# One 512-column product in place of two of 256 columns in the last feed-forward

## The chip, the cores and the metric

The kernel runs on one core of a Trainium2 chip. The metric is the device time of one execution in microseconds (us). A program of this kind repeats within about 0.1%: the three runs of the kernel before lie between 2305.07 and 2306.84 us. A nanosecond (ns) is a thousandth of a microsecond; durations of single instructions are given in ns.

The engines are named as the profile names them: PE is TensorE's matrix product and PEld its weight load, DVE is VectorE, ACT is ScalarE, POOL is GpSimd, SP is SyncE, whose queue here issues the DMAs.

## The reference

A two-layer trunk works on two groups of 128 tokens of width 2048, a context pass and a denoising step, with the same weights. Each layer is a mixer (attention) followed by a gated feed-forward with a width-3 convolution over the tokens. The change is in the feed-forward of the second, last layer:

```
def conv_ffn(h, w_up, w_conv, b_conv, w_down):
    u = h @ w_up                                   # 2048 -> 2 * 5632
    up = jnp.pad(u, ((0, 0), (1, 1), (0, 0)))
    u = up[:, :-2] * w_conv[0] + up[:, 1:-1] * w_conv[1] + up[:, 2:] * w_conv[2] + b_conv
    gate, val = u[..., :D_FF], u[..., D_FF:]
    return (jax.nn.silu(gate) * val) @ w_down      # 5632 -> 2048
...
x = x + gt2 * conv_ffn(h, ...)
```

All of it is float32.

## The kernel before

The two groups lie side by side: every product has 2 x 128 = 256 token columns (`NT`), and features stand on the 128 partitions. A weight matrix is cut into blocks of 128 x 128. One output chunk of 128 features is the sum over all blocks of its row of weights: 16 blocks for the up-projection (2048 inputs), 22 for one half of the down-projection (the 5632 inputs are done in two halves, `NQ = 2`).

A product in full float32 is made of three products in a faster format, `fp32r`. Each weight is split into a high part `wh` (ACT casts it, L248) and the rest `wl` (DVE subtracts, L249), and so is each operand: its high half lies in columns 0 to 255 of a 512-column row, its low half in columns 256 to 511. `gemm` then adds three products of 256 columns for each block into one PSUM tile `acc` of 128 x 512, of which it uses the first half: `wh` times the high half, `wh` times the low half, `wl` times the high half. Every product loads its weights anew. `acc` has three buffers, `raw` (the weights as they come from memory, 1 MB) three, `wh` and `wl` four each, every one with 8 blocks.

`ffn` runs, for each half `q` of the 5632 features, `up(q)` and then `down(gs, q)`. `up` takes 22 pairs of chunks (gate and value). `conv` asks `product()` for a chunk and makes the convolution of it: ACT scales and shifts it out of PSUM into `cv` (L1531), and DVE adds the two neighbours with two operations that read PSUM (L1534, L1537). Then ACT takes the SiLU of the gate, DVE multiplies (L1554), and the result is split into the high and low half of `g`. `down` makes 16 chunks of 22 blocks each, and `residual` (L843) or, for the very last chunk, `last_residual` (L827) adds them to `x` with DVE, straight from PSUM.

In the last feed-forward the first four chunks of `up` are ready before: they were made from the raw operand while the norm's factor was still being computed, three products of 258 columns to a block ("raw chunks"). `product()` hands them out first. Then come some chunks in an order written out by hand (`in_order`, with `keep_order`), and then five chunks whose first product is widened by 32, 16, 8, 4 and 2 columns (`WIDER`), the extra columns being thrown away. All the others use plain `gemm`.

Beside the products of `up(0)` DVE also works through rows of `w_ada` for the modulation vectors: long reductions at L473, which `pump` hands out at a rate (`FRATE`). The order of instructions on each engine is otherwise set by a scheduler with its own timing model, from the order of the code.

At the end, after the last chunk of `down(1)`, the last squares, the norm's factor and the scaling of `x` follow, one after the other, and the output goes out.

Of the kernel before, what the change touches and what calls it, by code (L numbers as in the profile page):

```python
# [14 lines left out]
ALU = mybir.AluOpType  # L15
# [3 lines left out]
P = 128  # L19
# [3 lines left out]
NT = 2 * T  # L23
ROW = 2 * NT
SHIFT = 320
NL = 2
# [68 lines left out]
def step_kernel(ctx: ExitStack, tc: tile.TileContext, A: dict):  # L95
    nc = tc.nc
    dve, act, pool, sp = nc.vector, nc.scalar, nc.gpsimd, nc.sync
    kept = []

    def keep_order(i):  # L100
        if not any(i is j for j in kept):
            kept[:] = [i]
            tc.keep_in_program_order(i)
# [16 lines left out]
    pe = TensorE()  # L120
# [5 lines left out]
    pacc = ctx.enter_context(tc.tile_pool(name="pacc", bufs=3, space=PSUM))  # L126
# [5 lines left out]
    def banks(name):  # L132
        return tc.tile_pool(name=name, bufs=1, space=PSUM)
# [3 lines left out]
    def nm(s):  # L137
        uid[0] += 1
        return f"{s}_{uid[0]}"

    def T_(pl, shape, tag, dt=F32, bufs=None):
        kw = {} if bufs is None else {"bufs": bufs}
        return pl.tile(shape, dt, tag=tag, name=nm(tag), **kw)
# [103 lines left out]
    def split(out_hi, out_lo, src, pin=lambda i: i):  # L247
        pin(act.copy(out_hi, src))  # L248
        pin(dve.tensor_tensor(out=out_lo, in0=src, in1=out_hi.bitcast(F32), op=ALU.subtract))  # L249
# [102 lines left out]
        return [p[:, :NT] for p in ps]  # L352

    push = []

    def gemm(blocks, xh, xl, n=NT, first=0, between=None, more=None, wider=None):

        fixed = lambda i: keep_order(i) if between is not None else i  # L360
        ps = T_(pacc, [P, 512], "acc")
        last = len(blocks) - 1
        for i in range(last + 1):
            k = (i + first) % (last + 1)
            wh, wl = blocks[k]
            x0 = more(k) if more and i == 0 else wider(k, 0, n + push.pop(0)) if push else xh(k)
            fixed(pe.matmul(ps[:, :x0.shape[-1]], wh, x0, start=(i == 0), stop=False,
                            skip_group_check=i > 0 and x0.shape[-1] > n))
            if callable(between):
                if i == (last + 1) // 2:  # L370
                    between()
            elif between and i in between:
                between[i]()
            x1 = wider(k, NT, n + push.pop(0)) if push else xl(k)
            fixed(pe.matmul(ps[:, :x1.shape[-1]], wh, x1, start=False, stop=False, skip_group_check=x1.shape[-1] > n))
            fixed(pe.matmul(ps[:, :n], wl, xh(k), start=False, stop=(i == last)))
        return ps[:, :n]
# [81 lines left out]
    def load_row():  # L459
        feat["row"] = T_(feat["home"], [P, 2, D], "condb")  # L460
        sp.dma_start(out=feat["row"], in_=A["condb"])
        for r in range(2):
            keep_order(act.activation(feat["row"][:, r], feat["row"][:, r], AF.Silu))
# [30 lines left out]
    class Deep:  # L494
# [44 lines left out]
        def pump(self):  # L539
            self.due += self.rate  # L540
            while self.due >= 1.0:
                self.due -= 1.0
                if self.steps:
                    self.step()
# [82 lines left out]
    def ensure(l, j, qs=range(4)):  # L627
        for u in [(l, j, q) for q in qs]:
            while u in ROWS and u not in done and ada["i"] <= ROWS.index(u):
                row_step()  # L630
            while u in FEATS and u not in done:
                feature_step()
            while u in DEEP[l] and u not in done:
                deep.step()
            while u not in done:
                later.pop(0)()
# [95 lines left out]
    def raw_tile(pl, tag):  # L732
        return home(pl, tag)[:, :KD * 2 * UW].rearrange("p (k n) -> p k n", k=KD)
# [766 lines left out]

    def ffn(hx, W, ready, turn, l, st):
        xh, xl = (lambda k: hx[:, k, :NT]), (lambda k: hx[:, k, NT:2 * NT])
        wider = list(WIDER)
        long = len(ready) > 3

        def product():
            if ready:
                return ready.pop(0)
            if in_order:
                return gemm(W.chunk(), xh, xl, between=in_order.pop(0))  # L1510
            if wider:
                n = NT + wider.pop(0)
                return gemm(W.chunk(), xh, xl, more=lambda k: hx[:, k, :n])
            return gemm(W.chunk(), xh, xl)

        WD = Weights(A["w_down"][l], KQ, TB)
        cw = ada["cw"]
        with tc.tile_pool(name=f"ffn{l}", bufs=1) as fp, banks(f"pffn{l}") as pf:
            feat["home"], feat["pool"] = fp, pf
            feat["due"] = 0.0  # L1520
            in_order = [{}, {}] + turn + [{}]
            T_(fp, [P, SHIFT // 4], "pad")

            def conv(m):
                early = bool(ready)
                pin = keep_order if early else lambda i: i
                if len(ready) > 4 - 2 * long:
                    W.ahead(pin)
                ps = product()
                y = T_(fp, [P, NT], "cv", bufs=3)  # L1530
                pin(act.activation(y, ps, AF.Identity, scale=cw[:, 1, m:m + 1], bias=cw[:, 3, m:m + 1]))  # L1531
                y3 = y.rearrange("p (g t) -> p g t", g=2)
                p3 = ps.rearrange("p (g t) -> p g t", g=2)
                pin(dve.scalar_tensor_tensor(out=y3[:, :, 1:], in0=p3[:, :, :T - 1],  # L1534
                                             scalar=cw[:, 0, m:m + 1], in1=y3[:, :, 1:],
                                             op0=ALU.mult, op1=ALU.add))
                pin(dve.scalar_tensor_tensor(out=y3[:, :, :T - 1], in0=p3[:, :, 1:],  # L1537
                                             scalar=cw[:, 2, m:m + 1], in1=y3[:, :, :T - 1],
                                             op0=ALU.mult, op1=ALU.add))
                if early and ready and not long:  # L1540
                    W.ahead(pin)
                return y

            def up(q):
                gs = []
                for i in range(q * KQ, (q + 1) * KQ):
                    rate = 0 if i < LATE else FRATE["up"]
                    fine[0] = False
                    gate = conv(i)
                    pump(0, rate)  # L1550
                    val = conv(NFF + i)
                    pump(0, rate)
                    act.activation(gate, gate, AF.Silu)
                    dve.tensor_tensor(out=val, in0=gate, in1=val, op=ALU.mult)  # L1554
                    g = T_(fp, [P, ROW], "g", F32R, bufs=KQ)
                    split(g[:, :NT], g[:, NT:2 * NT], val)
                    gs.append(g)
                    if i == LATE - 1:
                        load_row()
                return gs  # L1560

            def down(gs, q):
                u, rows = None, None
                if q == NQ - 1 and l < NL - 1:
                    u = raw_tile(keep, "hx")
                    rows = raw_rows(u, l + 1, 0)
                for c in range(KD):
                    quiet = q == NQ - 1 and c >= KD - QUIET[0]
                    fine[0] = quiet
                    if q == 0:  # L1570
                        ensure(l, 5, [c // 4])
                    ps = gemm(WD.chunk(), lambda k: gs[k][:, :NT], lambda k: gs[k][:, NT:2 * NT])
                    if l == NL - 1 and q == NQ - 1 and c == KD - 1:
                        last_residual(ps, l, 1, c, st)
                    else:
                        residual(ps, l, 1, c, st if q == NQ - 1 else None)
                    if rows:
                        rows(c)
                    if l == NL - 1 and q == NQ - 1 and c in EARLY:
                        act.activation(x[:, c], x[:, c], AF.Identity, scale=C("gfin")[:, c:c + 1])  # L1580
                    pump(0, 0 if quiet else FRATE["down"])
                return u

            for q in range(NQ):
                gs = up(q)
                u = down(gs, q)
            while feat["i"] < FLIMIT[stage[0]]:
                feature_step()
            return u


    with banks("pab") as ppool["ada"]:
# [3 lines left out]
        ps = T_(pacc, [P, 512], "acc")  # L1596
# [5 lines left out]
        hx = operand(keep, "hx")  # L1602
        st = stat_init()
        with tc.tile_pool(name="beside", bufs=1) as beside:
            o = mixer_ab(hx, beside)
            with tc.tile_pool(name="raw", bufs=1) as rp:
# [3 lines left out]
                W = Weights(A["w_up"][0], KD, 1)  # L1610
# [5 lines left out]
    with tc.tile_pool(name="cc", bufs=1) as cp, banks("pc") as ppool["ada"]:  # L1616
# [3 lines left out]
        W = Weights(A["w_in_c"], KD, 1)  # L1620
# [5 lines left out]
        W = Weights(A["w_up"][1], KD, 1)  # L1626
# [154 lines left out]
```

## Time and profile before

| what | value |
|---|---|
| median of three runs | 2306.41 us (2305.07 to 2306.84) |
| span of the profiled execution | 2305.7 us |
| PE busy | 2275.9 us, 99% |
| DVE busy | 1885.6 us, 82% |
| ACT busy | 1195.7 us, 52% |
| last feed-forward, from its first plain chunk to its last product | about 1596 to 2293 us of the span |
| after the last product | about 12 us |

The span is that of one profiled execution, which stands for its own time here; the runs are other executions, and their median is 0.7 us above the span. A row of a timeline gives the start of an instruction or of a group that was merged, how long it took, and xcount; the pace of products is read from the distance between starts, since each product's own duration (276 ns for one of 256 columns) overlaps the next. Rows of groups give busy time, the mean ns of one, and the idle time of the engine just before them with what ended it.

### The profile page before, as it was taken

Reading aid. Unit: us, or ns where it says so; the run is one execution under the profiler, and the core shown is the slowest. Engines: PE = TensorE matmul, PEld = TensorE weight load, DVE = VectorE, ACT = ScalarE, POOL = GpSimd, SP = SyncE. Lnnn points to the kernel's source line nnn. Section 1 sums busy time; section 2 is a strip of 40 time slices with the busy share of each in tenths; the row PEclk is TensorE's granted clock in tenths of the full one; section 3 lists DMA queues with packets and bytes.
Section 4 is the critical chain, followed back from the end, with each engine's and each line's share of the span. In section 5 each row is a group of like instructions: output and inputs, shape, how many; then the busy total and the mean of one; then the engine's idle time right before and its main releaser. Section 6 shows DMA issues by size and latency. Waiting matters only on the chain.

```text
span 2305.7 us, 47484 instructions
## 1 busy us (share of the span) xinstructions
PE 2275.9 (99%) x19496; PEld 2182.1 (95%) x19496; DVE 1885.6 (82%) x2973; ACT 1195.7 (52%) x1959; POOL 188.1 (8%) x238
## 2 busy tenths in 40 slices
PE   8999999999999999999999999999999999999998
PEld 6788878999999999999999999999999999999998
DVE  4667979989999999999978988898899965666654
ACT  4345555665553355555575455457555434555543
POOL 0002111300000000001130001023000000000011
PEclk9999999999999999999999999999999999999999
DMA  9987888777777777777788888776667755555553
GB/s 376 367 343 293 326 311 338 288 277 264 262 255 291 291 272 260 272 258 258 288 293 293 318 322 310 267 268 229 246 256 262 264 200 189 199 191 194 198 189 126
DMA packets 100122, 617.15 MB, mean 268 GB/s; under 512 B 10752, under 2 KB 18880, under 8 KB 33344
## 3 DMA queue, kind: packets, MB, share of 16 engines
q1 hardware_dynamic: 99904, 614.11, 72.2%
q8 instruction: 153, 2.51, 0.4%
q14 instruction: 65, 0.53, 0.1%
HBM read 609.32 MB, written 4.75 MB: 266 GB/s over the span
## 4 chain that ended last, share of the span: by engine, by line
PE 93%; DVE 3%; DMA 2%; issue 1%; POOL 1%; ACT 1%; SPq 0%; DVEq 0%; ACTq 0%; POOLq 0%
PE acc L110 86%; PE ada L110 3%; PE att L110 2%; DVE wl L249 1%; DVE hx L525 1%; DMA more<-w_ada 1%; PE att L113 1%; DMA raw<-w_out_c 0%; PE misc L110 0%; DMA araw<-w_ada 0%; DMA kvb<-w_ada 0%; POOL dev L807 0%; PE ada L113 0%; DVE rope L858 0%; ACT wh L248 0%
## 5 line engine op out<-in xcount | busy, mean ns | idle before, releaser
L110 PE MATMUL acc<-hx,wh 128*128 128x256 f32 (+1 forms) x7264 | 1255.2, 278 | 4.2 <-ACT wh L248 1.7
L248 ACT CAST wh<-raw 128x1024 fp32r<-128x1024 f32 (+1 forms) x834 | 796.6, 967 | 869.8 <-PE acc L110 736.6
L249 DVE TENSOR_TENSOR wl<-raw,wh 128x1024 fp32r<-128x1024 f32 (+1 forms) x834 | 925.4, 1126 | 246.9 <-ACT wh L248 240.2
L110 PEld LDWEIGHTS acc<-hx,wh 128*128 128x128 f32 x7264 | 1099.8, 188 | 23.2 <-ACT wh L248 8.1
L110 PE MATMUL acc<-hx,wl 128*128 128x256 f32 (+1 forms) x3632 | 1007.8, 278 | 5.3 <-DVE wl L249 5.1
L110 PEld LDWEIGHTS acc<-hx,wl 128*128 128x128 f32 x3632 | 684.5, 188 | 9.5 <-DVE wl L249 6.9
L110 PE MATMUL acc<-g,wh 128*128 128x256 f32 x2816 | 478.8, 276 | 0.0
L110 PEld LDWEIGHTS acc<-g,wh 128*128 128x128 f32 x2816 | 424.0, 188 | 0.0
L110 PE MATMUL acc<-g,wl 128*128 128x256 f32 x1408 | 388.1, 276 | 0.0
L473 DVE CUSTOM_DVE_ANT_0 junk<-araw,condb 128x2048 f32<-128x2048 f32 x128 | 294.4, 2300 | 0.0
L110 PEld LDWEIGHTS acc<-g,wl 128*128 128x128 f32 x1408 | 264.2, 188 | 0.0
L211 POOL TENSOR_TENSOR sqacc<-sqacc,sq 128x256 f32<-128x256 f32 x62 | 71.5, 1154 | 1491.1 <-ACT sq L207 1490.9
L110 PE MATMUL acc<-hxc,wh 128*128 128x256 f32 (+1 forms) x1056 | 189.3, 281 | 0.0
L110 PEld LDWEIGHTS acc<-hxc,wh 128*128 128x128 f32 x1056 | 161.9, 188 | 1.8 <-issue 1.7
L110 PE MATMUL acc<-hxc,wl 128*128 128x256 f32 (+1 forms) x528 | 146.9, 278 | 0.0
L110 PEld LDWEIGHTS acc<-hxc,wl 128*128 128x128 f32 x528 | 99.6, 189 | 0.2
L110 PE MATMUL acc<-wh,hxc 128*128 128x256 f32 (+1 forms) x512 | 95.0, 283 | 0.5 <-DVE nt L818 0.5
L1531 ACT ACTIVATE cv<-acc,convw 128x256 f32<-128x256 f32 x169 | 94.1, 557 | 0.0
L525 DVE CUSTOM_DVE_ANT_0 hx<-block,condb 128x1024 fp32r<-128x1024 f32 x65 | 79.3, 1221 | 7.3 <-DMA block<-w_ada 6.8
L1537 DVE SCALAR_TENSOR_TENSOR cv<-acc,convw,cv 128x254 f32<-128x254 f32 x169 | 81.1, 480 | 3.2
L843 DVE SCALAR_TENSOR_TENSOR x<-acc,mod,x 128x128 f32<-128x128 f32 x190 | 57.3, 344 | 31.6 <-PE acc L110 31.6
L110 PEld LDWEIGHTS acc<-wh,hxc 128*128 128x128 f32 x512 | 79.4, 188 | 3.4 <-issue 2.5
(263 smaller groups left out, 1800.4 us busy)
## 6 DMA issues: line engine op xcount, KB each, us to landing
raw<-w_up SPq DMA_DIRECT2D x176, 1024.0 KB, 4.8
araw<-w_ada SPq DMA_DIRECT2D x136, 1024.0 KB, 6.0
raw<-w_down SPq DMA_DIRECT2D x88, 1024.0 KB, 4.8
raw<-w_in_c SPq DMA_DIRECT2D x48, 1024.0 KB, 6.9
block<-w_ada SPq DMA_DIRECT2D x41, 512.0 KB, 6.8
raw<-w_in_ab SPq DMA_DIRECT2D x18, 1024.0 KB, 9.1
raw<-w_out_ab SPq DMA_DIRECT2D x16, 1024.0 KB, 7.9
raw<-w_out_c SPq DMA_DIRECT2D x16, 1024.0 KB, 7.1
```

The costliest lines, as they stand in the source:

```text
L110: return self.placed(nc.tensor.matmul(*a, **kw))
L113: return self.placed(nc.tensor.transpose(*a, **kw))
L211: eng.tensor_tensor(out=st["acc"], in0=st["acc"], in1=sq, op=ALU.add)
L248: pin(act.copy(out_hi, src))
L249: pin(dve.tensor_tensor(out=out_lo, in0=src, in1=out_hi.bitcast(F32), op=ALU.subtract))
L473: keep_order(dve.tensor_tensor_reduce(out=T_(feat["pool"], [P, D], "junk"), in1=feat["row"][:, c], in0=feat["raw"].rearrange("p g n -> p ( ...
L525: keep_order(dve.tensor_tensor_reduce(out=self.junk, in0=self.raw, in1=self.row[:, c].rearrange("p (g n) -> p g n", g=2), scale=1.0, scala ...
L843: dve.scalar_tensor_tensor(out=x[:, c, s], in0=ps[:, s], scalar=mod[:, l, 3 * which + 2, c, g:g + 1], in1=x[:, c, s], op0=ALU.mult, op1=AL ...
L1531: pin(act.activation(y, ps, AF.Identity, scale=cw[:, 1, m:m + 1], bias=cw[:, 3, m:m + 1]))
L1537: pin(dve.scalar_tensor_tensor(out=y3[:, :, :T - 1], in0=p3[:, :, 1:], scalar=cw[:, 2, m:m + 1], in1=y3[:, :, :T - 1], op0=ALU.mult, op1=A ...
```

## The change

In the last layer (`wide = l == NL - 1`), every chunk that is not one of the four raw ones is made by a new function, `both_gemm`. For each block it makes one product of `wh` with all 512 columns of the operand's row, high and low half together, and one of `wl` with the high half. The first half of `acc` then holds the sum of two of the three parts and the second half the third part. So two operations follow each chunk: ACT copies the second half of `acc` to SBUF (`low`), and DVE adds it to the first half (`total`, also in SBUF, under the same tag with two buffers). What follows reads `total` where it read PSUM. The widened products (`WIDER`) are no longer made in the last layer, since `product()` returns before it comes to them.

```
    def both_gemm(blocks, both, xh, between=None):
        fixed = lambda i: keep_order(i) if between is not None else i
        ps = T_(pacc, [P, 512], "acc")
        last = len(blocks) - 1
        for k, (wh, wl) in enumerate(blocks):
            fixed(pe.matmul(ps, wh, both(k), start=(k == 0), stop=False, skip_group_check=True))
            if between and k in between:
                between[k]()
            fixed(pe.matmul(ps[:, :NT], wl, xh(k), start=False, stop=(k == last), skip_group_check=True))
        return ps
...
     def ffn(hx, W, ready, turn, l, st):
         xh, xl = (lambda k: hx[:, k, :NT]), (lambda k: hx[:, k, NT:2 * NT])
+        wide = l == NL - 1
...
             if in_order:
+                if wide:
+                    return both_gemm(W.chunk(), lambda k: hx[:, k, :2 * NT], xh, between=in_order.pop(0))
                 return gemm(W.chunk(), xh, xl, between=in_order.pop(0))
+            if wide:
+                return both_gemm(W.chunk(), lambda k: hx[:, k, :2 * NT], xh)
             if wider:
...
+                made = wide and not ready
                 ps = product()
+                if made:
+                    low = T_(fp, [P, NT], "low", bufs=2)
+                    act.copy(low, ps[:, NT:])
+                    total = T_(fp, [P, NT], "low", bufs=2)
+                    dve.tensor_tensor(out=total, in0=ps[:, :NT], in1=low, op=ALU.add)
+                    ps = total
                 y = T_(fp, [P, NT], "cv", bufs=3)
...
-                    ps = gemm(WD.chunk(), lambda k: gs[k][:, :NT], lambda k: gs[k][:, NT:2 * NT])
+                    if wide:
+                        ps = both_gemm(WD.chunk(), lambda k: gs[k][:, :2 * NT], lambda k: gs[k][:, :NT])
+                        low = T_(fp, [P, NT], "low", bufs=2)
+                        act.copy(low, ps[:, NT:])
+                        total = T_(fp, [P, NT], "low", bufs=2)
+                        dve.tensor_tensor(out=total, in0=ps[:, :NT], in1=low, op=ALU.add)
+                        ps = total
+                    else:
+                        ps = gemm(WD.chunk(), lambda k: gs[k][:, :NT], lambda k: gs[k][:, NT:2 * NT])
```

On DVE, here is a stretch in the middle of `up(0)` of the kernel before: the convolution of two chunks (`cv<-acc`), splits of weights (`wl`), one of the reductions for the modulation (`junk`).

```order
L1534 SCALAR_TENSOR_TENSOR cv_20391<-acc_20342,convw_14569,cv_20391 128x2x127
L249 TENSOR_TENSOR wl_20535<-raw_20532,wh_20534 128x1024
L249 TENSOR_TENSOR g_20329<-cv_20321,g_20329 128x256
L1537 SCALAR_TENSOR_TENSOR cv_20391<-acc_20342,convw_14569,cv_20391 128x2x127
L249 TENSOR_TENSOR wl_20539<-raw_20532,wh_20538 128x1024
L1534 SCALAR_TENSOR_TENSOR cv_20454<-acc_20405,convw_14569,cv_20454 128x2x127
L1537 SCALAR_TENSOR_TENSOR cv_20454<-acc_20405,convw_14569,cv_20454 128x2x127
L473 ISA junk_20460,mod_77<-araw_20458,condb_19923 128x2048
L473 ISA mod_77 128x1
```

The same place of the changed kernel (its line numbers are 13 to 25 higher there):

```order
L1553 TENSOR_TENSOR low_20332<-acc_20297,low_20330 128x256
L249 TENSOR_TENSOR wl_20514<-raw_20511,wh_20513 128x1024
L1559 SCALAR_TENSOR_TENSOR cv_20334<-low_20332,convw_14569,cv_20334 128x2x127
L1562 SCALAR_TENSOR_TENSOR cv_20334<-low_20332,convw_14569,cv_20334 128x2x127
L486 ISA junk_20340,mod_77<-araw_20338,condb_19899 128x2048
L486 ISA mod_77 128x1
L1579 TENSOR_TENSOR cv_20334<-cv_20283,cv_20334 128x256
L1553 TENSOR_TENSOR low_20392<-acc_20357,low_20390 128x256
L249 TENSOR_TENSOR wl_20518<-raw_20511,wh_20517 128x1024
```

One addition for each chunk has come in (`low<-acc,low`), ahead of the two operations that now read its result.

At the end of the program, ACT's rows of the kernel before (the squares of the last chunks, `sq`, and the copy of the norm's factor, `nt`):

```order
L1580 ACTIVATE x_76<-x_76,cst_74 128x256
L248 CAST wh_28040<-raw_28032 128x512 x2
L207 ACTIVATE sq_28029<-x_76 128x256
L830 ACTIVATE sq_28113<-x_76 128x128 x2
L1641 COPY nt_28134<-misc_28131 128x256
```

and of the changed kernel:

```order
L248 CAST wh_26474<-raw_26466 128x512 x2
L1600 COPY low_26457<-acc_26412 128x256
L207 ACTIVATE sq_26463<-x_76 128x256
L1600 COPY low_26525<-acc_26480 128x256
L843 ACTIVATE sq_26529<-x_76 128x128 x2
L1674 COPY nt_26550<-misc_26547 128x256
```

A copy for each of the last two chunks now stands between the last product and the squares.

More of the change, by code (lines that the diff above doesn't have):

```diff
@@ L354, in step_kernel, with both_gemm @@
     push = []
+    def both_gemm(blocks, both, xh, between=None):
+        fixed = lambda i: keep_order(i) if between is not None else i
+        ps = T_(pacc, [P, 512], "acc")
+        last = len(blocks) - 1
+        for k, (wh, wl) in enumerate(blocks):
+            fixed(pe.matmul(ps, wh, both(k), start=(k == 0), stop=False, skip_group_check=True))
+            if between and k in between:
+                between[k]()
+            fixed(pe.matmul(ps[:, :NT], wl, xh(k), start=False, stop=(k == last), skip_group_check=True))
+        return ps
     def gemm(blocks, xh, xl, n=NT, first=0, between=None, more=None, wider=None):
```

## The prediction

> **What bounds the kernel now.** The first question is which engine the last feed-forward waits for. I read the page's part 1, its chain, then the table of stages and the list of waits for this part of the span.
>
> ```profile
> PE 2275.9 (99%) x19496; PEld 2182.1 (95%) x19496; DVE 1885.6 (82%) x2973; ACT 1195.7 (52%) x1959; POOL 188.1 (8%) x238
> ...
> PE 93%; DVE 3%; DMA 2%; issue 1%; POOL 1%; ACT 1%; SPq 0%; DVEq 0%; ACTq 0%; POOLq 0%
> ```
>
> PE carries 93% of the chain. The table of stages (columns: time, then busy time and instructions of PE, PEld, DVE, ACT, POOL, then the granted clock, the share of the DMA engines and GB/s) shows most of `up(0)`, and then the end of `down(0)`, `up(1)` and `down(1)`:
>
> ```profile
> 1640.00:1820.00 180.00, 180.00 (x1591) 180.00 (x1590) 167.62 (x217) 95.78 (x133) 0.00 (x0) 1.00 0.72 262
> 1880.00:2292.00 412.00, 412.00 (x3638) 412.00 (x3637) 251.49 (x337) 200.41 (x267) 16.50 (x14) 1.00 0.53 185
> ```
>
> PE never pauses, at full granted clock (1.00). But DVE has only 180 - 167.6 = 12.4 us free in the first row. The waits of PE from 1595 us to the end are two, both behind the last chunk:
>
> ```profile
> PE misc L110 <- POOL rr L222: 1.0, 1, 1.0
> PE misc L110 <- ACT sq L830: 0.5, 1, 0.5
> ```
>
> So the time of this part is the number of products times their pace. The pace is read from starts in the timeline; each line is the `wl` product of a block, and the pairs stand 13 and 12 blocks apart:
>
> ```profile
> 1608.28 0.28 PE L110 MATMUL acc<-hx,wl 128*128 128x256 f32 x1
> ...
> 1612.87 0.28 PE L110 MATMUL acc<-hx,wl 128*128 128x256 f32 x1
> ...
> 1614.28 0.28 PE L110 MATMUL acc<-hx,wl 128*128 128x256 f32 x1
> ...
> 1618.36 0.28 PE L110 MATMUL acc<-hx,wl 128*128 128x256 f32 x1
> ```
>
> The same three products take 4.59 / 13 = 0.353 us until 1613 us and 4.08 / 12 = 0.340 us from 1614 us on: 117.7 and 113.3 ns for each. Between them lies the product widened by 32 columns. PE has two steady paces here, a slow and a fast one; the fast one holds to the end (412 us / 3638 products = 113.2 ns).
>
> **What a product of 512 columns costs.** No such product of split operands is in the trace. The nearest rows are the products of 384 columns in the first layer; these are starts of groups three products apart:
>
> ```profile
> 219.84 0.34 PE L110 MATMUL acc<-kv_in,wl 128*128 128x384 f32 x1
> ...
> 220.36 0.34 PE L110 MATMUL acc<-kv_in,wl 128*128 128x384 f32 x1
> ...
> 220.88 0.34 PE L110 MATMUL acc<-kv_in,wl 128*128 128x384 f32 x1
> ...
> 222.08 0.34 PE L110 MATMUL acc<-kv_in,wl 128*128 128x384 f32 x1
> ...
> 222.61 0.34 PE L110 MATMUL acc<-kv_in,wl 128*128 128x384 f32 x1
> ...
> 223.14 0.34 PE L110 MATMUL acc<-kv_in,wl 128*128 128x384 f32 x1
> ```
>
> Here too are two paces: 0.52 / 3 = 173.3 ns and 0.53 / 3 = 176.7 ns. So 128 columns more cost 173.3 - 113.3 = 60.0 ns in the fast pace and 59.0 in the slow one: 0.47 ns a column, more than the 113.3 / 256 = 0.44 of a whole product of 256. Nothing in these rows looks like a fixed price per product that a longer product would save. A straight line gives 233.3 ns for 512 columns at the fast pace, 235.7 at the slow one. The bounds come from mixing the paces: 384 fast less 256 slow gives 55.6 ns for 128 columns, 384 slow less 256 fast gives 63.4, so 512 columns cost between 229 and 240 ns by these rows.
>
> The Trainium skill says otherwise. Its page "TensorE: Matmul & The Clock Gate", section "Back-to-back issue gap", gives N / 2.4 + 2.5 ns between products of N columns at full clock. By that 384 columns take 162.5 ns, and the trace has 173.3; 256 take 109.2, and the trace has 113.3. The measurement decides; by the page's rule alone 512 columns would take 215.8 ns.
>
> **The change part by part.** The blocks concerned: 84 chunks of `up` (88 less the four raw ones) times 16, and 32 chunks of `down` times 22: 1344 + 704 = 2048.
>
> PE. Each block loses two products of 256 columns (226.7 ns at the fast pace) and gets one of 512 (233.3 ns): +6.7 ns, and 2048 x 6.7 = +13.7 us. I take the straight line at the fast pace, because the 384 rows are the nearest and the fast pace holds for all but the first three chunks of this part. By the bounds a block changes by +2 ns (229) to +13 (240); with both products at the slow pace it takes 235.7 + 117.7 = 353.4 ns, +13.4. PE loads one set of weights less per block; this is worth nothing in the sum, since at 384 columns the load has time to hide and the product is no cheaper by the column.
>
> ACT and DVE, for each of the 116 chunks: a copy of 256 columns out of PSUM and an addition. Their nearest rows are the copy at the end of the program, in the timeline, and the groups of DVE and ACT between 1640 and 1880 us (busy, mean ns of one, then idle before and its releaser):
>
> ```profile
> 2297.34 0.37 ACT L1641 COPY nt<-misc 128x256 f32<-128x256 f32 x1 [3.07 <-DVE x L1638]
> ```
>
> ```profile
> L249 DVE TENSOR_TENSOR wl<-raw,wh 128x1024 fp32r<-128x1024 f32 x88 | 105.8, 1223 | 21.3 <-ACT wh L248 21.0
> L473 DVE CUSTOM_DVE_ANT_0 junk<-araw,condb 128x2048 f32<-128x2048 f32 x30 | 68.8, 2292 | 0.0
> ...
> L1554 DVE TENSOR_TENSOR cv<-cv,cv 128x256 f32<-128x256 f32 x17 | 7.2, 422 | 0.1
> ...
> L248 ACT CAST wh<-raw 128x1024 fp32r<-128x1024 f32 x89 | 93.8, 1055 | 120.7 <-PE acc L110 104.4 <-ACT g L248 12.4 <-issue 3.9
> ```
>
> ACT: 0.37 us more for each chunk of about 5.5 us, and the activation that follows reads SBUF in place of PSUM:
>
> ```profile
> L1531 ACT ACTIVATE cv<-acc,convw x169: 546/557/564, 470.2 to 2174.5; 128x256 f32<-128x256 f32 x169
> ...
> L1531 ACT ACTIVATE cv<-nt,convw x7: 586/599/602, 462.7 to 1607.6; 128x256 f32<-128x256 f32 x7
> ```
>
> That is 42 ns more in the median. ACT is idle 120.7 us of those 240 ahead of its casts, 104.4 of them because PE has not yet freed a weight buffer. So both fit, and cost nothing while the casts run ahead of PE. The activation now waits for DVE's addition, and the casts queue up behind it on ACT. With four buffers of 8 blocks, 8 x 0.34 = 2.7 us each, a cast may come some 5 us late before PE stands still; the longest thing in front of the addition on DVE is one reduction (2.3 us) and one split (1.2 us). I put this wait at nothing.
>
> DVE: 33 chunks lie between 1640 and 1820 us, and 33 x 0.42 = 13.9 us meet 12.4 us of room. At today's pace DVE would be 1.5 us short there; at 346.7 ns a block the same chunks take 183.5 us and need 181.5. The reductions end at about 1830 us, and behind it DVE has room (251 of 412 us). I put down +0.5 us, between 0 and 4. The three PSUM buffers come free after the addition rather than after the second convolution step, so nothing is later there. On SP's queue a few loads of `w_ada` and of weights change places; no wait of PE in this part ends with a DMA, and with three raw tiles in flight I put this at nothing; a late weight tile would cost what is left of its load.
>
> The end. Behind the last product DVE began at once:
>
> ```profile
> 2293.30 0.02 issue
> 2293.32 0.36 DVE x L827
> ```
>
> Now a copy (0.37) and an addition (0.42) stand in between, which nothing covers, with a handoff of 0.02: +0.8 us.
>
> The lost `WIDER`. No widened product now pushes the products out of the slow pace in which the chunk before 1613 us ran. Whether 512 and 256 in turn fall into the fast pace by themselves, no row shows. This is the second rival.
>
> The sum on the profiled execution: 2305.7 + 13.7 + 0.5 + 0.8 = 2320.7 us; the median of the runs lies 0.7 above its span, so 2321.4, say 2321.
>
> **The rivals.** First, faster: a fixed price per product is saved. The two paces differ by 4.4 ns for one and the same product of 256 columns, so some of its time isn't streaming; if that much is paid once per product and 512 columns cost 226.7 - 4.4 = 222.3 ns, then 2048 x 4.4 = 9.0 us are gained, DVE's shortage in `up(0)` takes about 2 back, and the end 0.8: 2305.7 - 9.0 + 2.0 + 0.8 + 0.7 = 2300 us. It decides from 512 columns under 224 ns on. Against it stand the 384 rows, by which 512 columns cost at least 229.
>
> The page's rule belongs here as well: with 215.8 ns, 10.9 less than now, a block would gain 22 us in all, about 2287 us with DVE's shortage; since it is 10.8 ns off at 384 columns, I give that end little.
>
> Second, slower still: the blocks stay in the slow pace. Then 2048 x 13.4 = 27.4 us come on top, DVE has room, and the time is 2305.7 + 27.4 + 0.8 + 0.7 = 2335 us. For it: the slow pace held for some three whole chunks by itself until the widened product came, and that product is gone. Against it: after it the fast pace held for 680 us, through every change from `up` to `down`.
>
> Third, no change on PE: a product of 512 columns costs just twice one of 256, 226.7 ns. Then 2305.7 + 0.8 + 1.5 (DVE) + 0.7 = 2309 us. For it: a stall that comes once in 256 columns would fit; against it: 384 columns would then take 170, not 173.3.
>
> Fourth, the chain ACT copy, DVE addition, ACT activation makes the casts late in `up(0)`: if each of the 40 chunks beside the reductions lost 0.5 us, 20 us, to 2327 or more. The 104 us in which casts wait for PE speak against it.
>
> **How the numbers follow.** Straight line at the fast pace 0.40; slow pace 0.22; no change on PE 0.17; fixed price saved 0.17 (the page's end of it 0.04 of these); late casts 0.04. What a measurement tells from no change is about 0.2%, 4.6 us. So: slower 0.40 + 0.22 + 0.04 = 0.66, same 0.17, faster 0.17. The time is that of the straight line, 2321 us; its own range, from block changes of +4 to +9 ns, is 2315 to 2326. The range goes down to 2298, so that it takes in the cases of no change and the nearer half of the faster one, and up to 2337, which takes in the slow pace; outside it are the rest of the faster case and late casts on top of a slow pace, some 0.15.
>
> **What the changed profile would show.** The starts of two `wl` products of neighbouring blocks lie 0.347 us apart (0.353 in the slow pace, 0.340 with no change, under 0.337 if faster). PE is still busy without a pause from 1596 us to the last product, some 14 us later than 2293; DVE shows close to 100% in `up(0)`; waits of PE for `wl` there would show the fourth rival. Between the last product and the first operation on `x` stand a copy and an addition, 0.8 us. The prediction is wrong above all if columns beyond 384 are cheaper than those up to it, or if a product of 512 changes the pace of the one of 256 beside it; the rows have no such alternation.

## The result and the profile after

The changed kernel takes 2339.93 us (median of four runs, 2338.99 to 2341.66) where the kernel before takes 2306.42. The ratio of the runs is 1.0151, interval 1.0136 to 1.0165; the two medians lie 33.5 us apart. The forecast was 2321 us with a range to 2337; the time lies just above the range, near the second rival (2335 us).

The span of the profiled execution is 2337.5 us, 31.8 more than before. The chain is still PE's, by engine:

```profile
PE 91%; DVE 4%; DMA 3%; issue 1%; ACT 1%; POOL 1%; SPq 0%; DVEq 0%; ACTq 0%; POOLq 0%
```

The pace of the blocks, in the timeline of PE; the two lines lie 11 blocks apart:

```profile
2000.29 0.28 PE L110 MATMUL acc<-hx,wl 128*128 128x256 f32 x1
2000.41 0.40 PE L110 MATMUL acc<-hx,wh 128*128 128x512 f32 x1
...
2004.18 0.28 PE L110 MATMUL acc<-hx,wl 128*128 128x256 f32 x1
```

3.89 / 11 = 0.3536 us a block: the 353.4 ns that the prediction gave for the slow pace, not the 346.7 of its forecast. It is the same from the first block of this part to the last, apart from the blocks at a wait. Beside it, the two stages and the list of PE's waits from 1595 us to the end:

```profile
1640.00:1820.00 180.00, 178.26 (x1008) 154.19 (x1006) 169.41 (x235) 100.56 (x157) 0.00 (x0) 1.00 0.69 249
1900.00:2320.00 420.00, 420.00 (x2379) 364.79 (x2378) 272.11 (x399) 217.51 (x331) 17.12 (x14) 1.00 0.53 179
```

```profile
PE acc L110 <- DVE low L1602: 2.3, 1, 2.3
PE acc L110 <- DVE low L1553: 1.7, 3, 0.6
PE misc L110 <- ACT sq L843: 1.4, 1, 1.4
PE misc L110 <- POOL rr L222: 1.0, 1, 1.0
```

PE is no longer busy without a pause in `up(0)` (178.3 of 180 us): three times, 0.6 us each, it waits for DVE's addition into `low` (L1553) to give back a PSUM buffer. A fourth wait, 2.3 us, lies in `down(0)`, whose addition is L1602. Together they are 4.0 us; the two other waits are those of the end. On DVE the addition stands behind a reduction in all three waits of `up(0)` (the first is shown), and behind two splits in `down(0)`:

```profile
1694.82 2.29 DVE L486 CUSTOM_DVE_ANT_0 junk<-araw,condb 128x2048 f32<-128x2048 f32 x1
...
1697.03 0.42 DVE L1553 TENSOR_TENSOR low<-acc,low 128x256 f32<-128x256 f32 x1
...
1846.72 2.36 DVE L249 TENSOR_TENSOR wl<-raw,wh 128x1024 fp32r<-128x1024 f32 x2 [1.55 <-ACT wh L248]
1849.00 0.42 DVE L1602 TENSOR_TENSOR low<-acc,low 128x256 f32<-128x256 f32 x1
```

What stands between the last product and the residual, in the chain:

```profile
2323.87 0.02 issue
2323.89 0.02 ACTq L1600
2323.91 0.04 issue
2323.95 0.38 ACT low L1600
2324.33 0.02 issue
2324.35 0.44 DVE low L1602
2324.79 0.02 issue
2324.82 0.36 DVE x L840
```

From 2323.87 to 2324.82 it is 0.95 us, where DVE began 0.02 us after the last product before. The sum: 2048 blocks at 0.3534 us are 723.8 us, against 48 at 0.353 and 2000 at 0.340, 696.9, before: +26.9. With 4.0 for the waits and 0.9 for the end it is 31.8 us, the whole difference of the spans. That it closes so well is partly luck. Read from start to start, the four waits cost 5.0 us, 1.0 more than PE's idle time: the products around a wait of 0.58 us start 0.81 us later than they would without it. Against that, this execution came to its first plain chunk 0.9 us earlier (1595.1 in place of 1596.0 us).

### The profile page after: what moved, and what is told of

It is laid out like the page before. It is cut to its first block, busy times and chain, and to the rows that moved or that the text cites. A ratio compares the mean times of both kernels' runs of the same rounds, so it can differ in the third digit from the quotient of the medians.

```text
span 2337.5 us, 43713 instructions
## 1 busy us (share of the span) xinstructions
PE 2300.1 (98%) x17448; PEld 2111.1 (90%) x17448; DVE 1929.2 (83%) x3089; ACT 1231.2 (53%) x2075; POOL 188.3 (8%) x238
## 4 chain that ended last, share of the span: by engine, by line
PE 91%; DVE 4%; DMA 3%; issue 1%; ACT 1%; POOL 1%; SPq 0%; DVEq 0%; ACTq 0%; POOLq 0%
PE acc L110 86%; PE ada L110 3%; PE att L110 1%; DMA kvb<-w_ada 1%; DVE hx L538 1%; DVE wl L249 1%; DMA block<-w_ada 1%; PE att L113 0%; DMA araw<-w_ada 0%; PE misc L110 0%; ACT wh L248 0%; POOL dev L820 0%; PE ada L113 0%; DVE rope L871 0%; ACT p L888 0%
## 5 line engine op out<-in xcount | busy, mean ns | idle before, releaser
L110 PE MATMUL acc<-hx,wh 128*128 128x256 f32 (+2 forms) x5920 | 1269.8, 305 | 6.7 <-DVE low L1553 1.7
L110 PEld LDWEIGHTS acc<-hx,wh 128*128 128x128 f32 x5920 | 945.1, 188 | 88.8 <-issue 8.9
L110 PE MATMUL acc<-g,wh 128*128 128x256 f32 (+1 forms) x2112 | 488.1, 316 | 2.3 <-DVE low L1602 2.3
L110 PEld LDWEIGHTS acc<-g,wh 128*128 128x128 f32 x2112 | 344.1, 188 | 35.1 <-DVE low L1602 2.7
L110 PE MATMUL ada<-araw,condw 128*32 128x512 f32 (+1 forms) x608 | 77.2, 596 | 2.8 <-DMA araw<-w_ada 2.7
L110 PE MATMUL acc<-wl,hxc 128*128 128x256 f32 x256 | 71.3, 279 | 0.0
L538 DVE CUSTOM_DVE_ANT_0 hx<-more,condb 128x1024 fp32r<-128x1024 f32 x42 | 51.2, 1220 | 4.8 <-DMA more<-w_ada 4.3
```

Of the source, the lines that this page charges most:

```text
L110: return self.placed(nc.tensor.matmul(*a, **kw))
L538: keep_order(dve.tensor_tensor_reduce(out=self.junk, in0=self.raw, in1=self.row[:, c].rearrange("p (g n) -> p g n", g=2), scale=1.0, scala ...
```

## The experiments

Two questions were open. Why are the blocks in the slow pace: because the push by the widened product is lost, or because of the 512 columns? And what do 512 columns cost by themselves?

### Products of 256 columns without the push

The kernel before, with the widened products left out of the last layer:

```
-        wider = list(WIDER)
+        wider = [] if l == NL - 1 else list(WIDER)
```

> The kernel before, all products of 256 columns, but without the five widened products in the last feed-forward. Theory A (the last feed-forward starts in the slow pace, and only the widened product takes it out): the three products of a block take 0.353 us to the end, about 2000 x 13.3 ns = 27 us more, 2333 us. Theory B (the slow pace gives way to the fast one by itself, at the latest where up changes to down; the changed kernel is slow for its 512 columns alone): 0.340 us from some point on, 2306 to 2320 us.

Measured: 2331.80 us, ratio 1.0118 (1.0088 to 1.0147), 26.0 us slower. Theory A held. In the timeline of PE, again 11 blocks:

```profile
2000.30 0.28 PE L110 MATMUL acc<-hx,wl 128*128 128x256 f32 x1
...
2004.18 0.28 PE L110 MATMUL acc<-hx,wl 128*128 128x256 f32 x1
```

3.88 / 11 = 0.353 us: the slow pace lasts for 720 us, through every change between `up` and `down`. So the missing push alone costs 26 us, and three products of 256 columns at the slow pace take just as long as one of 512 and one of 256.

### The changed kernel with a push

```
+            n = NT + (more if k == 0 else 0)
-            fixed(pe.matmul(ps[:, :NT], wl, xh(k), start=False, ...))
+            fixed(pe.matmul(ps[:, :n], wl, both(k)[:, :n], start=False, ...))
```

where `more` is 32, 16, 8, 4 and 2 for five chunks.

> The changed kernel, with the wl product of the first block of five chunks widened by 32, 16, 8, 4 and 2 columns into the second half (its low-by-low terms are added, which the reference has too). Theory A (the changed kernel lost only the push; a 512 and a 256 product have a fast pace too, by the straight line 346.7 ns a block): about 2000 x 6.7 = 13 us less than the changed kernel's 2340, 2326 us. Theory B (512 and 256 in turn have one pace only, the slow one): 353.4 ns a block and 2340 us.

Measured: 2341.81 us, ratio 1.0161 (1.0132 to 1.0191), 0.353 us a block throughout. As theory B has it; but a push on the `wl` product proved weak below (run with 256 columns in both halves), so this run alone does not exclude theory A.

### 512 columns in `down` alone

Only `down` uses `both_gemm`, with the copy and the addition; `up` is that of the kernel before, push and all.

> The 512-column products in down alone (704 blocks); up is that of the kernel before, with its widened products, so down is entered at the fast pace. Theory A (the pace is kept, 346.7 ns a block): 704 x 6.7 = 4.7 us and 0.8 at the end more than before, 2312 us. Theory B (the alternation falls to 353.4 ns by itself): 704 x 13.4 = 9.4 and 0.8, 2317 us. up(1), between the two downs, is at 340 ns by A; by B the question is whether it comes back to 340.

Measured: 2327.36 us, ratio 1.0098 (1.0069 to 1.0128). `up(0)` ends at 0.340 us a block; then the timeline of PE in `down(0)` and in `up(1)`, 8 and 12 blocks apart:

```profile
1900.04 0.28 PE L110 MATMUL acc<-g,wl 128*128 128x256 f32 x1
...
1902.87 0.28 PE L110 MATMUL acc<-g,wl 128*128 128x256 f32 x1
...
2100.03 0.28 PE L110 MATMUL acc<-hx,wl 128*128 128x256 f32 x1
...
2104.27 0.28 PE L110 MATMUL acc<-hx,wl 128*128 128x256 f32 x1
```

0.354 us in `down`, though it was entered at the fast pace: the alternation falls back by itself. And 0.353 in `up(1)`, whose products are the plain ones: once lost, the fast pace doesn't come back here. Theory A fell; theory B held for `down` and had left `up(1)` open: its 2317 us and 704 x 13.3 ns = 9.4 us for `up(1)` make the 2327 that was measured.

### Only products of 512 columns in `down`

```
-            fixed(pe.matmul(ps[:, :NT], wl, xh(k), start=False, ...))
+            fixed(pe.matmul(ps, wl, both(k), start=False, ...))
```

> As the run with 512 columns in down alone, but there the wl product takes all 512 columns as well (it adds the low-by-low term), so down has products of 512 columns only. It measures what 512 columns cost beside their like. Theory A (straight line at the fast pace, 233.3 ns): 466.7 ns a block, 704 x 126.7 = 89 us more, 2396 us. Theory B (slow pace, 235.4 ns as in the changed kernel): 470.8 ns, 92 us more, 2399 us. At just twice a 256 product, 226.7 ns, it would be 453.4 ns and 2387 us.

Measured: 2395.51 us, ratio 1.0394 (1.0364 to 1.0424). Timeline of PE in `down(0)`, 7 blocks:

```profile
1899.64 0.40 PE L110 MATMUL acc<-g,wl 128*128 128x512 f32 x1
...
1902.90 0.40 PE L110 MATMUL acc<-g,wl 128*128 128x512 f32 x1
```

3.26 / 7 = 0.466 us a block, 233 ns for a product, and `up(1)` is at 0.340. So 512 columns among their like have the fast pace, and it costs what the straight line through 256 and 384 columns gave. A long product saves nothing: 233.3 is more than twice 113.3.

### The same products in groups

`down` alone again, but the 22 products of 512 columns of a chunk first and then its 22 of 256:

```
+        for k, (wh, wl) in enumerate(blocks):
+            keep_order(pe.matmul(ps, wh, both(k), start=(k == 0), ...))
+        for k, (wh, wl) in enumerate(blocks):
+            keep_order(pe.matmul(ps[:, :NT], wl, xh(k), ..., stop=(k == last), ...))
```

> As the run with 512 columns in down alone, but each chunk of down makes its 22 products of 512 columns first and then its 22 of 256, in that order. Theory C (only products of unequal length next to each other are held in the slow pace; among their like both have the fast one): 22 x (233.3 + 113.3) ns a chunk and some 30 ns lost at each change of length, so 704 x 6.7 = 4.7 us, 2 us for 64 changes and 0.8 at the end: 2313 us, and up(1) at 0.340 us a block. Theory D (one product of another length is enough to lose the fast pace until a widened product brings it back): 0.353 us a block in down and in up(1), 2327 us as in the run with 512 columns in down alone.

Measured: 2314.41 us, ratio 1.0046 (1.0026 to 1.0066). Timeline of PE, where a line is a whole group:

```profile
1906.15 5.29 PE L110 MATMUL acc<-g,wh 128*128 128x512 f32 x22
1911.28 2.66 PE L110 MATMUL acc<-g,wl 128*128 128x256 f32 x22
1913.78 5.29 PE L110 MATMUL acc<-g,wh 128*128 128x512 f32 x22
```

5.13 / 22 = 233.2 ns and 2.50 / 22 = 113.6 ns, 7.63 us a chunk: the changes of length cost nothing that can be seen, and `up(1)` keeps 0.340. Theory C held, theory D fell. That the time lies so near theory C's 2313 us is partly luck: no run shows its 30 ns for a change of length, and in place of these 2 us PE waits 2.5 us for the last `g` of `up`:

```profile
PE acc L110 <- DVE g L249: 2.5, 2, 1.8
```

The run with 512 columns in `down` alone has no such wait. `keep_order` fixes the order of PE's products in `down`, which the scheduler otherwise mixes, and that is the likely reason; no run tests it by itself. The same products with the same copies and additions as in `down` alone take 13 us less, for their order.

### Fewer reductions beside `up`

The changed kernel, with `pump`'s rate in `up` of the last layer at 0.45 in place of 0.7.

> The changed kernel, with the reductions for the modulation handed out in up of the last feed-forward at a rate of 0.45 in place of 0.7, so that DVE has room there. If PE's 4.0 us of waits for the addition into low come from DVE being full, they go, and the time is 2336 us. If they come from the three PSUM buffers or from the order of copy, addition and activation, they stay and the time is 2340 us.

Measured: 2333.53 us, ratio 1.0126 (1.0097 to 1.0155). The waits of PE from 1560 us to the end are only those of the end:

```profile
PE misc L111 <- ACT sq L844: 1.4, 1, 1.4
PE misc L111 <- POOL rr L223: 1.0, 1, 1.0
```

All four waits are gone. The time is 28.2 us above the kernel before beside it, in place of 33.5, and from the first product of this part to the last the trace is 5.1 us shorter: what the four waits cost from start to start. So the reductions beside `up` caused them. DVE was not full, though, as the expectation has it: in the changed kernel it was busy 169.4 of the 180 us, here 158.0. In `up(0)` it is enough that one reduction of 2.3 us stands ahead of an addition that is due. Why fewer of them also take away the wait in `down(0)`, behind two splits, is not shown. The blocks stay at 0.353.

### Copies and additions without the 512 columns

The changed kernel with three products of 256 columns, high by low into the second half of `acc`, and five widened `wl` products:

```
-            fixed(pe.matmul(ps, wh, both(k), start=(k == 0), ...))
+            fixed(pe.matmul(ps[:, :NT], wh, xh(k), start=(k == 0), ...))
+            fixed(pe.matmul(ps[:, NT:], wh, both(k)[:, NT:], start=False, ...))
-            fixed(pe.matmul(ps[:, :NT], wl, xh(k), ...))
+            fixed(pe.matmul(ps[:, :n], wl, both(k)[:, :n], ...))
```

> The changed kernel with three products of 256 columns to a block again (high by high and the wl product into the first half, high by low into the second) and all its copies and additions; five wl products are widened. It takes the length of the product away and leaves the rest. Theory C: fast pace, 0.340 us a block, and what is left is the copies and additions: 0.8 to 1.1 us at the end and 4 to 6 us of PE waiting for DVE in up(0), where the faster pace leaves DVE less room: 2311 to 2313 us. If copies and additions have a part in the slow pace (PSUM read while it is written): 0.353 us a block, 2338 us.

Measured: 2315.04 us, ratio 1.0066 (1.0033 to 1.0099); the medians lie 9.8 us apart. Six of its eight runs lie between 2312.8 and 2316.8 us, two at 2333.5 and 2335.5, about where a kernel that stays in the slow pace would be; there is no trace of these two. In the profiled one `up(0)` changes between the paces. The last block before a wait for `low`, the wait, and 6 blocks behind it:

```profile
1752.25 0.28 PE L110 MATMUL acc<-hx,wl 128*128 128x256 f32 x1
1752.96 0.50 PE L110 MATMUL acc<-hx,wh 128*128 128x256 f32 x2 [0.43 <-DVE low L1555]
1753.30 0.28 PE L110 MATMUL acc<-hx,wl 128*128 128x256 f32 x1
...
1755.34 0.28 PE L110 MATMUL acc<-hx,wl 128*128 128x256 f32 x1
```

Before the wait a block takes 0.353 us, after it 2.04 / 6 = 0.340. From the third such wait, at 1809 us, the fast pace holds to the end, with the copies and additions of all chunks beside it: these alone don't hold the blocks in the slow pace. A part they may still have. Twice in `up(0)` the fast pace was lost again, both times at the first block of a chunk, where PE came late right behind the addition that gave back the buffer, by 0.13 us at 1729.5 and by 0.02 us at 1769.4:

```profile
1729.11 0.42 DVE L1555 TENSOR_TENSOR low<-acc,low 128x256 f32<-128x256 f32 x1
```

```profile
1729.52 0.28 PE L110 MATMUL acc<-hx,wl 128*128 128x256 f32 x1
...
1729.99 0.28 PE L110 MATMUL acc<-hx,wl 128*128 128x256 f32 x1
```

This block takes 0.47 us in place of 0.34, and the next ones 0.353. So the fast pace came behind waits of 0.43 us and went behind small delays; no run takes this apart. Of the widened `wl` products, those of 32 and 4 more columns brought the fast pace, and at those of 8 and 2 it was lost again, within 30 blocks. The changed kernel has the same waits of 0.6 us and stays slow behind each.

### Other lengths beside 512

`down` alone, with `wl` products of 384, 320 and 288 columns.

> As the run with 512 columns in down alone, but there the wl product takes 384 columns (it adds part of the low-by-low term). It asks if any two unequal lengths run at the slow pace. Theory C (yes, at 0.461 ns a column as 512 beside 256 does): 412.6 ns a block, 704 x 72.6 = 51 us, up(1) stays slow (9.4 us) and 0.8 at the end: 2367 us. Theory E (256 beside 512 is a special case, and these two keep the fast pace): 233.3 + 173.3 = 406.7 ns a block, up(1) at 0.340: 2353 us.

> As the run with 512 and 384 columns in down, with 320 for the wl product (832 columns a block). So far all steady paces are the slow rate of 0.460 ns a column (3 x 256 columns in 0.3533 us), cut down to a whole number of steps of 6.67 ns for what repeats: 256 alone 17.7 steps, runs at 17; 384 26.5, at 26; 512 35.3, at 35; 512 and 384 61.8, at 61; 512 and 256 53.0, at 53. Theory F (this rule): 57.4 steps, so 57, 380.0 ns a block: 704 x 40 = 28.2 us and 0.8 at the end on 2305.3, 2334 us. Theory G (each product keeps the fast pace of its length by the straight line, and 256 beside 512 is a case of its own): 233.3 + 143.3 = 376.7 ns, 2332 us. Theory C (unequal lengths: slow rate): 382.8 ns and a slow up(1), 2346 us.

> The same with 288 columns for the wl product (800 a block). Theory F: 55.2 steps, so 55, 366.7 ns a block, 2325 us. Theory G: 233.3 + 128.3 = 361.7 ns, 2321 us. Theory C: 368.1 ns and a slow up(1), 2335 us.

Measured: 2352.53 us (ratio 1.0208, 1.0179 to 1.0238), 2331.19 (1.0115, 1.0085 to 1.0144) and 2327.81 (1.0100, 1.0071 to 1.0129). Timelines of PE, first 384 (12 blocks), then 320 (13) and 288 (13):

```profile
1899.95 0.39 PE L110 MATMUL acc<-g,wh 128*128 128x512 f32 x1
...
1904.83 0.39 PE L110 MATMUL acc<-g,wh 128*128 128x512 f32 x1
```

```profile
1899.94 0.39 PE L110 MATMUL acc<-g,wh 128*128 128x512 f32 x1
...
1904.79 0.39 PE L110 MATMUL acc<-g,wh 128*128 128x512 f32 x1
```

```profile
1899.86 0.39 PE L110 MATMUL acc<-g,wh 128*128 128x512 f32 x1
...
1904.67 0.40 PE L110 MATMUL acc<-g,wh 128*128 128x512 f32 x1
```

They give 4.88 / 12 = 0.407, 4.85 / 13 = 0.373 and 4.81 / 13 = 0.370 us a block, and `up(1)` comes back to 0.340 in all three. So 384 beside 512 takes just the sum of the two fast paces (theory E), and it is not unequal length as such that is slow. At 320 the block is faster than each theory had it, at 288 slower than each: the rule of whole steps (theory F) fell, and none is left that gives all these numbers.

### Pairs

`down` alone, in the order `wh`, `wh`, `wl`, `wl` over two blocks:

> As the run with 512 columns in down alone, in the order wh, wh, wl, wl for two blocks at a time, so that each product has one neighbour of its length. Theory F: what repeats is 1536 columns, 106.0 steps for two blocks, 353.3 ns a block, as without pairs, and up(1) stays slow: 2327 us. Theory C (equal neighbours run fast, unequal ones slow): about 350 ns a block, 2313 to 2324 us. If one equal neighbour is enough for the fast pace: 346.7 ns and 2312 us.

Measured: 2312.20 us, ratio 1.0030 (1.0016 to 1.0044). Timeline of PE, 12 blocks:

```profile
1899.98 0.62 PE L110 MATMUL acc<-g,wh 128*128 128x512 f32 x2
...
1904.14 0.62 PE L110 MATMUL acc<-g,wh 128*128 128x512 f32 x2
```

4.16 / 12 = 0.3467 us a block, and `up(1)` is at 0.340. One neighbour of its own length is enough. PE waits 1.2 us for the last `g` here too, with the same fixed order in `down`.

### Pairs in the whole of the last feed-forward

> The changed kernel with the order wh, wh, wl, wl for two blocks at a time, in up and down; no widened products. It asks if pairs leave the slow pace in which this part starts without a push. If they do: 346.7 ns a block, 2048 x 6.7 = 13.7 us, 0.9 at the end and 4 to 6 us of waits for the additions on 2305: 2324 to 2326 us. If up begins and stays at the slow pace (353.3 ns) as the kernel without widened products does: 2337 us. In neither case does it beat the kernel before, since 512 columns at 233.3 ns cost more than twice 113.3.

Measured: 2332.71 us, ratio 1.0120 (1.0103 to 1.0137). Timeline of PE in `up(0)`, 14 blocks, and the waits of PE from 1560 us on, without those of the end:

```profile
1649.94 0.62 PE L110 MATMUL acc<-hx,wh 128*128 128x512 f32 x2
...
1654.80 0.39 PE L110 MATMUL acc<-hx,wh 128*128 128x512 f32 x1
```

```profile
PE acc L110 <- DVE g L249: 8.1, 3, 6.1
PE acc L110 <- DVE low L1555: 1.7, 3, 0.6
```

4.86 / 14 = 0.347 us, without any push: pairs leave the slow pace by themselves. But the time is 27.7 us above the kernel before (2305.05 beside it), 7 to 9 more than expected. The profiled execution is the slowest of the four (2336.69 us), so its parts are added up by themselves: from the first product to the last it takes 723.6 us, 26.7 more than the kernel before (697.0). The pace is 13.0 of these. The waits for `g` and `low`, 9.8 us of idle time, cost 11.2 from start to start. Behind the longest of them, 6.1 us, PE comes back at half its clock; the stretch from 1836.6 to 1842.4 us, with the granted clock third from the end, and two groups of it:

```profile
1836.60:1842.40 5.80, 5.31 (x17) 4.59 (x18) 3.98 (x7) 1.42 (x2) 0.00 (x0) 0.51 0.52 181
```

```profile
1838.11 1.05 PE L110 MATMUL acc<-g,wh 128*128 128x512 f32 x2
...
1839.39 1.05 PE L110 MATMUL acc<-g,wh 128*128 128x512 f32 x2
```

Two blocks take 1.28 us there in place of 0.69. From 1837.09 to 1842.55 us 17 products take 5.5 us, where the fast paces give 3.0: 2.4 us. With 13.0 and 11.2 that is the whole. The waits for `g` can come from two things that this run changes together: DVE, which is busy 172.7 of 180 us in `up(0)`, and the fixed order of PE in `down`; the runs in groups and in pairs have shorter ones with the `up` of the kernel before. No kernel here beats the one before.

## Why the prediction was wrong, point by point

- **The pace of the blocks** is the step that failed: "I take the straight line at the fast pace, because the 384 rows are the nearest and the fast pace holds for all but the first three chunks of this part". The term of 13.7 us measured 26.9. The blocks ran at 353 ns, the slow pace, which the prediction had priced right and given 0.22. Two of its sentences pointed there: that no widened product would push any more, and that no row showed an alternation of 512 and 256. The first is worth 26 us even with plain products; the second is the stronger reason, since the alternation falls from the fast pace by itself. The second rival's 2335 us were not the time either: it said that DVE has room, and the waits cost 5.0 us.
- **The straight line** for 512 columns was right: 233.3 ns, measured among its like and in groups. The rule of the Trainium skill that the prediction names (page "TensorE: Matmul & The Clock Gate", section "Back-to-back issue gap") gives 215.8 ns; the section calls it the gap of an isolated product and states about 131 ns for 512 columns in a stream with weight loads. Neither is what these products take; the traces decide.
- **No fixed price per product** is saved, as the 384 rows said; the rival with a gain fell.
- **DVE in `up(0)`**: 0.5 us was put down, 0 to 4 given. PE's idle time was 1.7 us there, and 2.3 more in `down(0)`, where the prediction saw room; that the 4.0 in all touches the end of its range is luck. The room was worked out right (180 us against 181.5 needed); but at 353 ns a block even 187 us for the same 33 chunks did not prevent the waits. The sentence that failed is "so nothing is later there": work which fits on average still comes late, a late addition holds a PSUM buffer, and PE stands still for it although casts and weights are ready. Nor do the reductions of the kernel before end at about 1830 us: five more start behind it, the last at 1850.3. The run with fewer reductions took all the waits away.
- **The end**: 0.8 put down, 0.95 less 0.02 measured; the ACT handoff (0.08 us) was missing.
- **Late casts** did not come; PE never waited for `wl` in this part.

What stays open is why 512 beside 256 in strict turn can't hold the fast pace, while 512 beside 384, or the same two lengths in pairs, can. The paces are measured; the mechanism behind them isn't.

## What to carry to other kernels

Ask for the pace of a stream of products from starts in the timeline, not from their durations, and look for more than one steady pace of the same instruction: here 113.3 and 117.8 ns for one shape are worth 26 us. Before two products are merged into a longer one, compare the price by the column at two lengths that the trace already has; if the longer is dearer, the rows give no reason to hope for a fixed price that is saved; here none was. And a change that takes out an odd-looking helper (a product that is a few columns too wide) is to be priced with the state that the helper set up.

## What the runs showed of the hardware

The steady paces of these products, all at full granted clock: 256 columns 113.3 or 117.8 ns, 384 columns 173.3 or 176.7, 512 columns 233.3; in strict turn, 512 with 256 353 ns for the two, with 288 370, with 320 373, with 384 407; in pairs, 512 with 256 346.7. Behind a turn of 512 with 256 the fast pace of 256 columns did not come back (0.353 us a block through all of `up(1)`); behind a turn with 288, 320 or 384, or behind pairs or groups, it did. Among products of 256 columns, one of 288 brought it, and so did waits of PE of 0.43 us; it went behind delays of 0.13 and 0.02 us. Pairs find it without a push. And behind a wait of PE of 6.1 us the granted clock was 0.50 until about 1842 us, 5 us on, with products of 512 columns 0.43 us apart.
